# Loads of the late modulation one step ahead, a fifth raw buffer, and earlier splits of weight tiles

## The chip, the cores and the metric

The kernel runs on one core of a Trainium2 chip. The metric is the device time of one execution in microseconds; the time of a kernel is the median of its runs. Engine names: TensorE (PE in the profile; PEld is its load of the stationary operand), VectorE (DVE), ScalarE (ACT), GpSimd (POOL, not used here) and SyncE (SP, which only issues DMAs here).

## The reference

One layer of a diffusion backbone in float32, for 256 latent tokens x and 256 context tokens, model width 2048. A conditioning vector c gives six modulation rows of 2048, three for the mixer and three for the feed-forward part:

```
sh_m, sc_m, g_m, sh_f, sc_f, g_f = split(silu(c) @ w_ada + b_ada, 6)
h = rmsnorm(x, norm_mix_w) * (1 + sc_m) + sh_m
p = h @ w_in                       # 2048 x 13376: x, B, C, dt | z | pool | fourier | three gates
merged = g0 * pool(p) @ w_pool * pool_scale + g1 * fourier(p) @ w_fourier + g2 * ssd(p) @ w_ssd_out
x = x + g_m * (merged @ w_out)
h2 = rmsnorm(x, norm_ffn_w) * (1 + sc_f) + sh_f
x = x + g_f * ((silu(h2 @ w_gate) * (h2 @ w_up)) @ w_down)     # d_ff = 5632
out = rmsnorm(x, final_norm_w)
```

`ssd` is a bidirectional Mamba-2 scan (32 heads of 64, state 128, chunks of 128) that starts from the context's final states; `pool` is a box mean over a 4 x 64 grid with windows 2 to 16; `fourier` is the real part of a two-dimensional DFT over positions and channels of a group.

## The kernel before, in words

**Products in three parts.** Each float32 operand is split into a high part (a cast to fp32r) and a low part (the rest). A product is three matmuls, high by high, high by low and low by high (L143 to L145). Weights come in tiles of 512 KB, two blocks of 128 rows by 512 columns, into a `raw` tile (L128 `stage_raw`). ScalarE casts the high half `whi` (L124), VectorE subtracts to get the low half `wlo` (L125), and twelve 128x512 matmuls use the tile. There are four `raw` buffers and three each of `hi` and `lo`. `raw` buffers are also used for the tiles of w_ada, for `stage_h` (L913) and for the last pieces of the down product (L1021).

**Stages.** Up to some 135 us the kernel computes the mixer's modulation, normalises and modulates the tokens and projects B, dt and the first columns of x. Then comes the mixer, whose steps are written in the string `ORDER`: u and P (pooling), x, c, s (SSD of one of four groups), z (its gate), F and f (Fourier), p, Y, q. After it come the output projection, the second norm (`norm_ffn`, L883) with the order on TensorE written out by hand, five rounds of `gate_up` (L972), a `down` over what they made, and so on to the last norm.

**The late modulation.** Of the six modulation rows, four (SC_F, SH_F, G_M, and later G_F) aren't needed by the mixer. `ada_rest` (L344) is a generator that computes them beside the projections: one step loads a 512 KB tile of w_ada, 128 rows by 1024 columns, into a `raw` buffer and adds it, scaled by a column of silu(c), to an accumulator `adacc` on VectorE (L355; the first of sixteen steps is a plain product). Sixteen steps make one half of a row; then follow a split, a sum over partitions on TensorE, and a bias. There are 96 steps for the first three rows, and 32 for G_F, which starts in `gate_up(0)`. `proj` and the other projections call `bg(n)` after each weight tile; n is a fraction from the table `BG`, and one step is run when the fractions reach one, so about every second or third weight tile.

**What sets the order.** The kernel's code gives the program order, and a scheduler that runs before the launch orders the instructions of TensorE, VectorE, ScalarE and SP from it: an instruction that comes earlier in the program has priority over a later one where both can be issued. Engines execute their instructions in the order that results. `load` (L97) issues a DMA on SP only after the last weight load in program order; weight loads themselves stay in their order. A load waits for the release of its buffer, and so do all loads behind it on SP. TensorE's order is fixed by hand only in the output projection and the norm behind it.

**The SSD step.** For each group, two halves of four heads (b) and two token tiles (t), `ssd` builds four `rh` tiles (L557 ScalarE, L559 VectorE), multiplies them with triangular constants (L560 `rh,gt_r` and `rh,lt_r`), takes the exponential E (L563), multiplies it into W (L569), multiplies W with x (L572 `W,xl`), adds the skip (L577 `yT`) and transposes the result (L582 `cc,yT`). `rh` has QR = 4 buffers. The Fourier step reads two tables (L97 `t<-ftab`), first used on TensorE at L796; the pooling step reads `ptab` (used at L759).

Of the kernel before, what the change touches and what calls it, by code (L numbers as in the profile page):

```python
# [11 lines left out]
F32 = mybir.dt.float32  # L12
# [52 lines left out]
WORK_AT = (0, 1, 8)  # L65
FETCH, STAGE, AT_W = 8, 1, 4

QR, QE = 4, 1
APART, APART2, TURNS0, TURNS1 = 3, 3, 1, 1
ORDER = "u P x0 c x1 u s0 x2 s1 z0 F x3 P z1 s2 p0 F z2 p1 f0 s3 z3 p2 f1 Y f2 p3 q0 f3 q1 q2 q3"  # L70
BG = {"x": 0.5, "z": 0.5, "u": 0.5, "p": 0.35, "F": 0.35, "f": 0.35, "q": 0.35, "s": 0.45}


@with_exitstack
def hybrid_block(ctx: ExitStack, tc, io):
# [51 lines left out]
    def stage_raw(src, n=CH):  # L127
        raw = wp.tile([P, 2, n], F32, tag="raw", name=nm("raw"), bufs=4)  # L128
        last[0] = nc.sync.dma_start(raw, src)
        return raw  # L130

    def stage(src, n=CH, raw=None):
        raw = raw or stage_raw(src, n)
        hi = wp.tile([P, 2, n], F32R, tag="hi", name=nm("whi"), bufs=3)
        lo = wp.tile([P, 2, n], F32R, tag="lo", name=nm("wlo"), bufs=3)
        split(hi, lo, raw)
        return hi, lo
# [8 lines left out]

    # ---------------------------------------------------------------- constants
    pp = C([P, PP_N], nme="pp")
# [40 lines left out]

    # ---------------------------------------------------------------- input norms  # L190
    xnT = [H([P, 2, CH], nme="xnT") for _ in range(8)]
# [37 lines left out]

    # ---------------------------------------------------------------- modulation of the mixer, B and dt  # L230
    Am = C([P, KT, 2], nme="Am")
# [58 lines left out]
    def project_bc(b):  # L290
        """B, dt and the first columns of x of quantum b, in steps"""
        hi, lo = stage(None, CH, w_raw[b][0])
        xhi, xlo = stage(None, 256, w_raw[b][1])
        yield

        def part(out, h, l, cs):
            for k in range(2):
                kt = 2 * b + k
                mm3(out, h[:, k, cs], l[:, k, cs], hh[b][:, k, :], hl[b][:, k, :], kt == 0, kt == KT - 1)

        for ct in range(4):
            part(bacc_[ct], hi, lo, slice(ct * P, (ct + 1) * P))
            yield
        for k in range(2):
            kt = 2 * b + k
            w = dtp[kt // 8][:, kt % 8, :]
            T.matmul(dtps, w, hh[b][:, k, :], start=kt == 0, stop=False)
            T.matmul(dtps, w, hl[b][:, k, :], start=False, stop=kt == KT - 1)
        yield
        for ct in range(2):  # L310
            part(xacc0[ct], xhi, xlo, slice(ct * P, (ct + 1) * P))
            yield
# [4 lines left out]
    nc.sync.dma_start(dtw, rows(w_in, 0, KT, DT_OFF, 64))  # L317
    # the parts of the columns of dt side by side: upper, lower
    dtp = [H([P, 8, P], F32R, nme="dtp") for _ in range(2)]
# [16 lines left out]

    # ---------------------------------------------------------------- background: rest of the modulation
    Af = C([P, KT], nme="Af")
# [4 lines left out]

    def ada_rest(offs):  # L344
        for off in offs:
            for half in range(2):
                a = wp.tile([P, 1024], F32, tag="adacc", name=nm("adacc"), bufs=1)
                for kt in range(KT):
                    raw = wp.tile([P, 1024], F32, tag="raw", name=nm("raw"), bufs=4)
                    c0 = off + half * 1024  # L350
                    load(raw, w_ada[kt * P : (kt + 1) * P, c0 : c0 + 1024])
                    if kt == 0:
                        V.tensor_scalar(a, raw, sil[:, kt : kt + 1], None, ALU.mult)
                    else:
                        V.scalar_tensor_tensor(a, raw, sil[:, kt : kt + 1], a, ALU.mult, ALU.add)  # L355
                    yield
# [40 lines left out]

    # ---------------------------------------------------------------- convolution
    def conv(dst, src, ct, ns):
        """dst, src: (P, ns, 256); depthwise taps of channel tile ct, then silu."""  # L400
        o = Q([P, ns, 256], nme="cv")
        w = [cwh[:, 5 * ct + k : 5 * ct + k + 1] for k in range(5)]
        S.activation(o, src, AF.Identity, bias=cwh[:, 120 + ct : 121 + ct], scale=w[2])
        for k in (1, 3, 0, 4):
            d = k - 2
            a, b = max(0, -d), 256 - max(0, d)
            V.scalar_tensor_tensor(o[:, :, a:b], src[:, :, a + d : b + d], w[k], o[:, :, a:b], ALU.mult, ALU.add)  # L407
        t = Q([P, ns, 256], nme="cvt")
        S.activation(t, o, AF.Tanh)
        V.scalar_tensor_tensor(dst, t, 1.0, o, ALU.add, ALU.mult)  # L410
# [7 lines left out]

    # ---------------------------------------------------------------- dt, decays
    def cs(ap):  # L420
# [56 lines left out]

    # ---------------------------------------------------------------- B, C
    BT = [H([P, 2, 2, 256], nme="BT") for _ in range(2)]
# [3 lines left out]

    # ---------------------------------------------------------------- SSD
    def bh(ap, n):
# [101 lines left out]

    # ---------------------------------------------------------------- token-major projections
    def h_op(kt, t):
# [154 lines left out]

    # ---------------------------------------------------------------- pooling
    dh, dl = [], []
# [25 lines left out]

    # ---------------------------------------------------------------- Fourier
    tabs = []
# [56 lines left out]

    # ---------------------------------------------------------------- output projection, residual
    def to_feature(chunks, scale=None, colscale=None):
        """(P, 2, CH) token-major chunks to split feature-major (P, 4, 256) tiles."""
        oh, ol = [], []
# [34 lines left out]
    def norm_ffn(t):  # L870
        """scales the rows of token tile t; returns four functions that turn and modulate them"""
        if t == 0:
# [37 lines left out]

    # the last columns and the first of the next product: the norm of one token tile under the products of the other
    def stage_h(w, p, c0):
        raw = wp.tile([P, 2, CH], F32, tag="raw", name=nm("raw"), bufs=4)  # L913
        hi, lo = H([P, 2, CH], F32R, nme="hhi"), H([P, 2, CH], F32R, nme="hlo")
# [53 lines left out]

    # ---------------------------------------------------------------- SwiGLU
    ah, al = [None] * NFC, [None] * NFC  # L970
# [33 lines left out]

    def down(n0, n1):
        for n in range(4):
            ps = proj(io["w_ffn_down"], 4 * n0, 4 * (n1 - n0), n * CH, pair_op(ah[n0:n1], al[n0:n1]))
# [11 lines left out]
    for n in range(4):  # L1019
        for p in range(2):  # L1020
            raw = wp.tile([P, 2, CH], F32, tag="raw", name=nm("raw"), bufs=4)  # L1021
            hi, lo = H([P, 2, CH], F32R, nme="dhi"), H([P, 2, CH], F32R, nme="dlo")
# [118 lines left out]
```

## Time and profile before

| what | value |
|---|---|
| runs | 1921.07, 1922.86, 1921.36 us |
| median | 1921.36 us |
| span of the profiled execution | 1922.6 us |
| granted TensorE clock, mean | 0.990 |
| HBM read | 405.56 MB, 212 GB/s over the span with what is written |

Times in the profile are microseconds from the start of the span. A row of a group gives line, engine, operation, output and inputs, the count, then busy time, mean nanoseconds of one, and the idle time just before with what ended most of it. A row of the waits gives who waited, for what, the total in us, how often, and the longest. A row of the windows gives a stretch, its length, the busy time of each engine with its count, the granted clock (1 is full speed), the share of DMA time and the rate. A row of the timeline gives start, duration, what ran, and in brackets the idle time before it and what ended it. Matmuls are pipelined, so the bars of two that follow overlap.

### The profile page before, as it was taken

The page shows a single profiled execution, that of the slowest core. Times are in us where ns is not written, and L with a number is a line of the kernel's source. Part 1 is how long each engine was busy: PE and PEld are TensorE (multiplying, and loading weights), DVE is VectorE, ACT ScalarE, POOL GpSimd, SP SyncE. Part 2 cuts the span into 40 slices and gives each one's busy share as a digit, 9 for nine tenths or more (in the row PEclk, how much of TensorE's full clock was granted, in tenths as well). Part 3 has the DMA queues.
Part 4 walks back from the last instruction along what each step waited for, and adds up shares of the span by engine and source line. Part 5 has one row for each costly group of instructions (what it writes and reads, how often), then busy time and mean ns, then how long its engine had stood idle before and what let it go on. Part 6 is the DMA issues. An engine that isn't in the chain of part 4 may idle for free.

```text
span 1922.6 us, 23276 instructions
## 1 busy us (share of the span) xinstructions
PE 1847.1 (96%) x8804; PEld 1483.4 (77%) x8804; DVE 1236.8 (64%) x1515; ACT 852.5 (44%) x1177; POOL 0.2 (0%) x4
## 2 busy tenths in 40 slices
PE   5999999999999999999999999999999999999998
PEld 3677886867777768777877887787788888888886
DVE  4338869695886687766656657666655555555567
ACT  5225535464464454533434544443343444433444
POOL 0000000000000000000000000000000000000000
PEclk8999999999999999999999999999999999999999
DMA  9985745454656747677777665787766666656655
GB/s 333 353 288 158 243 145 167 142 155 158 186 157 208 248 152 252 216 250 247 244 248 245 201 226 152 256 277 260 247 211 191 196 188 186 191 192 196 187 186 175
DMA packets 214081, 409.19 MB, mean 213 GB/s; under 512 B 14801, under 2 KB 51793, under 8 KB 213969
## 3 DMA queue, kind: packets, MB, share of 16 engines
q1 hardware_dynamic: 213968, 407.71, 67.1%
q8 instruction: 69, 1.13, 0.3%
q14 instruction: 44, 0.35, 0.1%
HBM read 405.56 MB, written 2.10 MB: 212 GB/s over the span
## 4 chain that ended last, share of the span: by engine, by line
PE 66%; DMA 17%; DVE 11%; issue 4%; ACT 2%; DVEq 0%; SPq 0%; ACTq 0%
PE acc L144 19%; PE acc L145 19%; PE acc L143 19%; DMA raw<-w_ada 14%; DVE wlo L125 5%; DVE adacc L355 2%; PE aux L262 1%; DVE cv L407 1%; PE aux L560 1%; DMA t<-ptab 1%; PE aux L522 1%; DMA raw<-w_in 1%; ACT whi L124 1%; PE aux L759 1%; DMA psc<-pool_scale 1%
## 5 line engine op out<-in xcount | busy, mean ns | idle before, releaser
L124 ACT CAST whi<-raw 128x1024 fp32r<-128x1024 f32 (+1 forms) x553 | 574.2, 1040 | 799.5 <-PE acc L145 554.2
L125 DVE TENSOR_TENSOR wlo<-raw,whi 128x1024 fp32r<-128x1024 f32 (+1 forms) x553 | 662.3, 1207 | 354.2 <-ACT whi L124 353.3
L144 PE MATMUL acc<-wlo,h2h 128*128 128x512 f32 x704 | 275.4, 391 | 2.5 <-DVE wlo L125 2.5
L143 PE MATMUL acc<-whi,h2h 128*128 128x512 f32 x704 | 275.0, 391 | 2.3 <-ACT h2h L124 2.3
L145 PE MATMUL acc<-whi,h2l 128*128 128x512 f32 x704 | 275.4, 391 | 0.0
L355 DVE SCALAR_TENSOR_TENSOR adacc<-raw,sil,adacc 128x1024 f32<-128x1024 f32 x120 | 154.0, 1283 | 176.1 <-DMA raw<-w_ada 175.8
L144 PE MATMUL acc<-wlo,lh 128*128 128x512 f32 x512 | 201.8, 394 | 5.4 <-DVE wlo L125 5.4
L143 PE MATMUL acc<-whi,lh 128*128 128x512 f32 x512 | 201.3, 393 | 0.0
L145 PE MATMUL acc<-whi,ll 128*128 128x512 f32 x512 | 200.6, 392 | 0.0
L144 PEld LDWEIGHTS acc<-wlo,h2h 128*128 128x128 f32 x704 | 132.4, 188 | 30.9 <-DVE wlo L125 3.8
L143 PEld LDWEIGHTS acc<-whi,h2h 128*128 128x128 f32 x704 | 132.3, 188 | 29.6 <-ACT h2h L124 2.7
L145 PEld LDWEIGHTS acc<-whi,h2l 128*128 128x128 f32 x704 | 132.5, 188 | 28.2 <-DVE h2l L125 1.3
L145 PE MATMUL acc<-whi,al 128*128 128x512 f32 x320 | 124.7, 390 | 0.0
L144 PE MATMUL acc<-wlo,ah 128*128 128x512 f32 x320 | 124.7, 390 | 0.0
L143 PE MATMUL acc<-whi,ah 128*128 128x512 f32 x320 | 124.6, 389 | 0.0
L144 PEld LDWEIGHTS acc<-wlo,lh 128*128 128x128 f32 x512 | 96.1, 188 | 29.9 <-DVE wlo L125 9.9
L145 PE MATMUL acc<-hh,wlo 128*128 128x512 f32 x288 | 113.8, 396 | 0.8 <-DVE wlo L125 0.8
L144 PE MATMUL acc<-hl,whi 128*128 128x512 f32 x288 | 114.5, 398 | 0.0
L143 PE MATMUL acc<-hh,whi 128*128 128x512 f32 x288 | 112.1, 402 | 0.9 <-ACT whi L124 0.9
L143 PEld LDWEIGHTS acc<-whi,lh 128*128 128x128 f32 x512 | 96.1, 188 | 20.7 <-issue 0.8
L145 PEld LDWEIGHTS acc<-whi,ll 128*128 128x128 f32 x512 | 96.1, 188 | 19.8 <-issue 0.2
L145 PEld LDWEIGHTS acc<-whi,al 128*128 128x128 f32 x320 | 60.1, 188 | 12.4
(294 smaller groups left out, 2467.8 us busy)
## 6 DMA issues: line engine op xcount, KB each, us to landing
raw<-w_in SPq DMA_DIRECT2D x200, 512.0 KB, 4.6
raw<-w_ada SPq DMA_DIRECT2D x192, 512.0 KB, 5.1
raw<-w_ffn_gate SPq DMA_DIRECT2D x88, 512.0 KB, 4.4
raw<-w_ffn_up SPq DMA_DIRECT2D x88, 512.0 KB, 4.4
raw<-w_ffn_down SPq DMA_DIRECT2D x88, 512.0 KB, 4.1
raw<-w_ssd_out SPq DMA_DIRECT2D x32, 512.0 KB, 4.9
raw<-w_out SPq DMA_DIRECT2D x32, 512.0 KB, 4.2
raw<-w_fourier SPq DMA_DIRECT2D x16, 512.0 KB, 4.5
```

Source lines behind the costliest of these rows:

```text
L124: S.copy(hi, src)
L125: V.tensor_tensor(lo, src, hi.bitcast(F32), ALU.subtract)
L143: T.matmul(out, ah, bh, start=first, stop=False)
L144: T.matmul(out, ah, bl, start=False, stop=False)
L145: T.matmul(out, al, bh, start=False, stop=last)
L262: T.matmul(ps[32 * k : 32 * k + 32, o], stat[:, 4 * p + k, :], raws[8 * j + i][:, k, :], start=p == 0, stop=p == 3)
L355: V.scalar_tensor_tensor(a, raw, sil[:, kt : kt + 1], a, ALU.mult, ALU.add)
L407: V.scalar_tensor_tensor(o[:, :, a:b], src[:, :, a + d : b + d], w[k], o[:, :, a:b], ALU.mult, ALU.add)
L522: T.matmul(ps, btk[:, 2 + t, :], xc[d][t], start=t == 0, stop=t == 1)
L560: T.matmul(seg, m, rh, start=n == 0, stop=n == 3)
L759: T.matmul(ps[:, k, :], u_pool[c][:, t, cc_ * P : (cc_ + 1) * P], tb[:, i, t, :], start=t == 0, stop=t == 1)
```

## The change

Five things, as they stand in the code:

1. The `raw` tag has five buffers, in all four places that allocate it.
2. `stage` puts its split under a scheduling priority 400 instructions ahead, so that the scheduler ranks it as if it stood that much earlier in the program. The splits of the late modulation, of `stage_h` and of the last pieces are not under it.
3. `ada_rest` asks for its tile one step ahead: the first step only loads, each later one loads the next tile and accumulates the one before.
4. `rh` has three buffers, and `BG["s"]`, the fraction in `gate_up`, goes from 0.45 to 0.48.
5. `down` runs what is left of the late modulation first.

```
-QR, QE = 4, 1
+AHEAD = 400
+QR, QE = 3, 1
...
-BG = {"x": 0.5, "z": 0.5, "u": 0.5, "p": 0.35, "F": 0.35, "f": 0.35, "q": 0.35, "s": 0.45}
+BG = {"x": 0.5, "z": 0.5, "u": 0.5, "p": 0.35, "F": 0.35, "f": 0.35, "q": 0.35, "s": 0.48}
...
-        raw = wp.tile([P, 2, n], F32, tag="raw", name=nm("raw"), bufs=4)
+        raw = wp.tile([P, 2, n], F32, tag="raw", name=nm("raw"), bufs=5)
...
-        split(hi, lo, raw)
+        with tc.high_priority(offset=AHEAD):
+            split(hi, lo, raw)
...
     def ada_rest(offs):
+        units = [(off, half, kt) for off in offs for half in range(2) for kt in range(KT)]
+        coming = []
+
+        def ask():
+            off, half, kt = units.pop(0)
+            c0 = off + half * 1024
+            coming.append(wp.tile([P, 1024], F32, tag="raw", name=nm("raw"), bufs=5))
+            load(coming[-1], w_ada[kt * P : (kt + 1) * P, c0 : c0 + 1024])
+
+        ask()
+        yield
         for off in offs:
             for half in range(2):
                 a = wp.tile([P, 1024], F32, tag="adacc", name=nm("adacc"), bufs=1)
                 for kt in range(KT):
-                    raw = wp.tile([P, 1024], F32, tag="raw", name=nm("raw"), bufs=4)
-                    c0 = off + half * 1024
-                    load(raw, w_ada[kt * P : (kt + 1) * P, c0 : c0 + 1024])
+                    if units:
+                        ask()
+                    raw = coming.pop(0)
                     if kt == 0:
...
     def down(n0, n1):
+        for _ in rest:
+            pass
```

The lines of the changed kernel are 1 to 13 higher than those of before (L355 becomes L368, L125 becomes L126, L560 becomes L573, L572 becomes L585, L582 becomes L595).

**VectorE in the late mixer,** in the first `ssd_out` step. Names end in the number of a buffer's tile; the same tile has a number smaller by one in the changed kernel. On SP the w_ada tile 7610 is loaded behind the weight tiles 7556, 7574 and 7592, and 7673 behind 7613, 7631 and 7655, in both kernels. Before:

```order
L355 SCALAR_TENSOR_TENSOR adacc_7369<-raw_7553,sil_96,adacc_7369 128x1024
L125 TENSOR_TENSOR wlo_7559<-raw_7556,whi_7558 128x1024
L125 TENSOR_TENSOR wlo_7577<-raw_7574,whi_7576 128x1024
L355 SCALAR_TENSOR_TENSOR adacc_7369<-raw_7610,sil_96,adacc_7369 128x1024
L125 TENSOR_TENSOR wlo_7595<-raw_7592,whi_7594 128x1024
L125 TENSOR_TENSOR wlo_7616<-raw_7613,whi_7615 128x1024
L355 SCALAR_TENSOR_TENSOR adacc_7369<-raw_7673,sil_96,adacc_7369 128x1024
L125 TENSOR_TENSOR wlo_7634<-raw_7631,whi_7633 128x1024
```

The same place in the changed kernel:

```order
L368 SCALAR_TENSOR_TENSOR adacc_7431<-raw_7552,sil_96,adacc_7431 128x1024
L126 TENSOR_TENSOR wlo_7558<-raw_7555,whi_7557 128x1024
L368 SCALAR_TENSOR_TENSOR adacc_7431<-raw_7609,sil_96,adacc_7431 128x1024
L126 TENSOR_TENSOR wlo_7576<-raw_7573,whi_7575 128x1024
L126 TENSOR_TENSOR wlo_7594<-raw_7591,whi_7593 128x1024
L126 TENSOR_TENSOR wlo_7615<-raw_7612,whi_7614 128x1024
L368 SCALAR_TENSOR_TENSOR adacc_7431<-raw_7672,sil_96,adacc_7431 128x1024
L126 TENSOR_TENSOR wlo_7633<-raw_7630,whi_7632 128x1024
```

The accumulation of tile 7610 (now 7609) stood behind the low half of 7574 and now stands before it. The load of 7673 waited for the buffer of 7610, four tiles before it; that of 7672 waits for the buffer of 7591, five tiles before it, which the low half two rows ahead of its accumulation frees.

**TensorE at the end of the SSD step s1.** `acc` rows are the projection that runs beside it; sixteen more of them stand between the last `rh,lt_r` and the first row here. Before:

```order
L143 MATMUL acc_3502<-whi_3638,hh_1205 128x512
L144 MATMUL acc_3502<-wlo_3639,hh_1205 128x512
L572 MATMUL aux_3251<-W_3308,xl_3094 64x128 x4
L145 MATMUL acc_3502<-whi_3638,hl_1206 128x512
L143 MATMUL acc_3502<-whi_3638,hh_1205 128x512
L144 MATMUL acc_3502<-wlo_3639,hh_1205 128x512
L145 MATMUL acc_3502<-whi_3638,hl_1206 128x512
L143 MATMUL acc_3503<-whi_3638,hh_1205 128x512
L582 MATMUL aux_3325<-cc_73,yT_3322 128x128
```

In the changed kernel:

```order
L146 MATMUL acc_3502<-wlo_3638,hh_1205 128x512
L147 MATMUL acc_3502<-whi_3637,hl_1206 128x512
L573 MATMUL aux_3286<-rh_3302,lt_r_112 128x512
L585 MATMUL aux_3250<-W_3307,xl_3093 64x128 x4
L595 MATMUL aux_3324<-cc_73,yT_3321 128x128 x4
L145 MATMUL acc_3722<-hh_379,whi_3728 128x512
L146 MATMUL acc_3722<-hl_380,whi_3728 128x512
```

The projection's matmuls that stood between the last three steps of the SSD are now ahead of them, and its last tile is through when the SSD's end begins.

**SP around the Fourier tables,** somewhat later in the same step. Before:

```order
L129 DMA raw_3796<-w_in 128x2x512
L97 DMA raw_3830<-w_ada 128x1024
L129 DMA raw_3833<-w_in 128x2x512
L97 DMA t_3657<-ftab 128x512
L97 DMA t_3658<-ftab 128x1024
L129 DMA raw_3865<-w_in 128x2x512
L97 DMA raw_3926<-w_ada 128x1024
```

In the changed kernel:

```order
L130 DMA raw_3795<-w_in 128x2x512
L98 DMA raw_3829<-w_ada 128x1024
L130 DMA raw_3832<-w_in 128x2x512
L130 DMA raw_3864<-w_in 128x2x512
L98 DMA raw_3898<-w_ada 128x1024
L130 DMA raw_3901<-w_in 128x2x512
L130 DMA raw_3933<-w_in 128x2x512
L98 DMA t_3656<-ftab 128x512
L98 DMA t_3657<-ftab 128x1024
```

Three weight tiles and one tile of w_ada now stand ahead of the tables that stood behind them.

More of the change, by code (lines that the diff above doesn't have):

```diff
@@ L912, in stage_h @@
     def stage_h(w, p, c0):
-        raw = wp.tile([P, 2, CH], F32, tag="raw", name=nm("raw"), bufs=4)
+        raw = wp.tile([P, 2, CH], F32, tag="raw", name=nm("raw"), bufs=5)
         hi, lo = H([P, 2, CH], F32R, nme="hhi"), H([P, 2, CH], F32R, nme="hlo")
@@ L1020, in hybrid_block @@
         for p in range(2):
-            raw = wp.tile([P, 2, CH], F32, tag="raw", name=nm("raw"), bufs=4)
+            raw = wp.tile([P, 2, CH], F32, tag="raw", name=nm("raw"), bufs=5)
             hi, lo = H([P, 2, CH], F32R, nme="dhi"), H([P, 2, CH], F32R, nme="dlo")
```

## Prediction

> **What bounds the kernel now.** I read the busy times first, then the costliest groups and the landing of the DMAs.
>
> ```profile
> span 1922.6 us, 23276 instructions
> ...
> PE 1847.1 (96%) x8804; PEld 1483.4 (77%) x8804; DVE 1236.8 (64%) x1515; ACT 852.5 (44%) x1177; POOL 0.2 (0%) x4
> ...
> L125 DVE TENSOR_TENSOR wlo<-raw,whi 128x1024 fp32r<-128x1024 f32 (+1 forms) x553 | 662.3, 1207 | 354.2 <-ACT whi L124 353.3
> ...
> L355 DVE SCALAR_TENSOR_TENSOR adacc<-raw,sil,adacc 128x1024 f32<-128x1024 f32 x120 | 154.0, 1283 | 176.1 <-DMA raw<-w_ada 175.8
> ...
> raw<-w_ada SPq DMA_DIRECT2D x192, 512.0 KB, 5.1
> ```
>
> TensorE is busy for 96% of the span, so whatever the change does to the loads, it can only move the other 4% and the stretches in which TensorE runs slowly. VectorE spends 176 us waiting for w_ada in front of the late modulation's accumulation (L355), a load that takes 5.1 us. That is the wait which the change goes for. How much of it reaches TensorE is the question, so the waits come next: one row of VectorE, then those of TensorE behind the first phase.
>
> ```profile
> DVE adacc L355 <- DMA raw<-w_ada: 175.8, 82, 4.9
> ...
> PE acc L144 <- DVE wlo L125: 16.3, 21, 1.7
> ...
> PE aux L992 <- DVE sg L985: 6.0, 4, 3.0
> PE aux L759 <- DMA t<-ptab: 5.8, 2, 3.5
> ...
> PE aux L522 <- DVE xc L516: 2.5, 1, 2.5
> ...
> PE aux L802 <- ACT pq L797: 2.2, 1, 2.2
> PE aux L368 <- ACT adasb L367: 2.2, 1, 2.2
> PE aux L796 <- DMA t<-ftab: 2.0, 1, 2.0
> ```
>
> 82 waits of VectorE, 175.8 us, leave 21 waits of TensorE for a low half (L125) and 16.3 us; four more (6.0 us) are for the SwiGLU's product on VectorE (L985). Seven eighths of VectorE's wait is hidden by split tiles in store. Last, the windows say where TensorE's idle time lies.
>
> ```profile
> core 0: us, PE busy (x) PEld busy (x) DVE busy (x) ACT busy (x) POOL busy (x), PEclk, DMA share, GB/s
> 135.00:300.00 165.00, 158.87 (x812) 133.09 (x805) 130.05 (x171) 77.43 (x110) 0.00 (x0) 0.98 0.59 179
> 300.00:440.00 140.00, 133.78 (x613) 99.46 (x612) 116.28 (x175) 77.56 (x162) 0.00 (x0) 1.00 0.51 153
> 560.00:700.00 140.00, 132.70 (x600) 104.40 (x599) 92.53 (x104) 57.16 (x78) 0.00 (x0) 0.99 0.69 219
> 800.00:1075.00 275.00, 266.14 (x1173) 215.91 (x1172) 170.99 (x164) 112.46 (x119) 0.00 (x0) 1.00 0.75 246
> 1180.00:1365.00 185.00, 176.45 (x780) 144.01 (x780) 126.13 (x121) 76.73 (x82) 0.00 (x0) 0.99 0.81 261
> 1365.00:1900.00 535.00, 535.00 (x2388) 442.31 (x2388) 301.09 (x294) 223.13 (x226) 0.00 (x0) 1.00 0.65 198
> ```
>
> From 1365 us on TensorE has no gap: 535 us in which nothing is to be had. TensorE's idle time, span less busy, is 6.1, 6.2, 7.3, 8.9 and 8.6 us in the five other windows, 37.1 us in all. This, with the half-speed stretches below, is the most that the change can bring.
>
> **How VectorE's wait becomes TensorE's.** The timeline around 879 us shows VectorE's rows, the issue of the load on SP, and TensorE's rows.
>
> ```profile
> 884.70 1.28 DVE L355 SCALAR_TENSOR_TENSOR adacc<-raw,sil,adacc 128x1024 f32<-128x1024 f32 x1 [4.61 <-DMA raw<-w_ada]
> 885.90 3.49 DVE L125 TENSOR_TENSOR wlo<-raw,whi 128x1024 fp32r<-128x1024 f32 x3
> ```
>
> ```profile
> 878.98 0.34 SPq L97 DMA_DIRECT2D raw<-w_ada  x1
> ```
>
> ```profile
> 885.71 0.39 PE L145 MATMUL acc<-whi,yl 128*128 128x512 f32 x1
> 885.94 0.39 PE L143 MATMUL acc<-whi,yh 128*128 128x512 f32 x1
> 887.17 0.50 PE L144 MATMUL acc<-wlo,yh 128*128 128x512 f32 x1 [0.84 <-DVE wlo L125]
> ```
>
> The load is issued at 878.98; VectorE, which runs its instructions in order, stands 4.61 us at the accumulation; three low halves are queued behind it and then run in one piece; TensorE stands 0.84 us at 887.17. Matmuls start 0.23 us apart (885.71, 885.94), so a weight tile, 12 of them, feeds TensorE for 2.8 us. One wait is hidden where the store is full, and shows where two follow closely.
>
> A second price hangs on TensorE's longer waits.
>
> ```profile
> 516.85:520.26 3.41, 3.41 (x8) 2.76 (x9) 1.92 (x3) 0.59 (x2) 0.00 (x0) 0.50 0.83 269
> 687.51:690.93 3.42, 3.08 (x4) 1.51 (x5) 3.42 (x6) 0.00 (x0) 0.00 (x0) 0.50 0.41 146
> 1359.94:1363.35 3.41, 3.41 (x13) 2.80 (x12) 2.58 (x5) 1.19 (x2) 0.00 (x0) 0.50 0.89 307
> ```
>
> In these windows, behind the ptab wait (up to 3.5 us), the xc wait (2.5) and the longest sg wait (3.0), the granted clock is 0.50 for 3.41 us: half of that, 1.7 us, is lost on top of the wait. The waits of 2.2 us (L802, L368) show none. [...]
>
> **The change, part by part.**
>
> *Asking one step ahead, fifth raw buffer.* The loads keep their order on SP almost everywhere, and so does the number of steps; BG["s"] moves from 0.45 to 0.48, which brings the G_F tiles a little earlier and costs nothing but DMA time where DMA is 0.81 busy. But the accumulation does not stand later on VectorE. In the late mixer the order shown above has it one weight tile earlier: it was behind two low halves of tiles loaded before it and is now behind one. The fifth buffer thus goes to weights, and a load whose buffer comes free one tile sooner is also used one tile sooner. Take the piece shown: the load of the third w_ada tile waits for the buffer of the weight tile split two places ahead of its accumulation. The loop is two low halves (2 x 1.2), a landing (5.1), an accumulation (1.3): 8.8 us, against three weight tiles of TensorE, 3 x 2.8 = 8.4. Where the loop carries two tiles (5.6), it does not fit at all, but neither did it before:
>
> ```profile
> 949.81 1.28 DVE L355 SCALAR_TENSOR_TENSOR adacc<-raw,sil,adacc 128x1024 f32<-128x1024 f32 x1 [4.17 <-DMA raw<-w_ada]
> 951.01 3.49 DVE L125 TENSOR_TENSOR wlo<-raw,whi 128x1024 fp32r<-128x1024 f32 x3
> 958.16 1.28 DVE L355 SCALAR_TENSOR_TENSOR adacc<-raw,sil,adacc 128x1024 f32<-128x1024 f32 x1 [3.65 <-DMA raw<-w_ada]
> ```
>
> From one accumulation to the next it is 8.35 us already. I put the excess of 0.4 us on about eight such loops: **+3** in 800 to 1075. Ends: -6 (two thirds of the window's 8.9 us idle goes) and +10 (0.84 us at each of a dozen accumulations).
>
> *Priority of the splits.* Splits go ahead of VectorE's and ScalarE's other work, so a tile loaded one earlier is also split earlier. This helps where the wait came from the mixer's other work. FFN window: of 8.6 us idle and 1.7 us of half clock at 1360 I take half: **-5** (ends 0 and -10). 560 to 700: 7.3 idle and 1.7 of half clock, the xc wait among them: **-5** (0 to -9). 135 to 440: 12.3 idle, of which the table and adasb waits stay: **-4** (0 to -8). What was late stays late for sg and xc if the splits now go ahead of these too, which is why I take half and no more. Together -14.
>
> *QR 4 to 3 and the order on TensorE.* The fourth rh tile must wait for the first, and with projections drawn forward nothing is left to stand between the end of s1 and the next gating. Before:
>
> ```profile
> 426.90 0.63 PE L560 MATMUL aux<-rh,lt_r 128*128 128x512 f32 x2
> 427.37 0.40 PE L145 MATMUL acc<-whi,hl 128*128 128x512 f32 x1
> ...
> 431.57 0.66 PE L572 MATMUL aux<-W,xl 128*64 128x128 f32 x8
> ...
> 433.44 0.27 PE L582 MATMUL aux<-cc,yT 128*128 128x128 f32 x1
> ```
>
> ```profile
> 427.63 0.60 ACT L563 ACTIVATE E<-aux 128x512 f32<-128x512 f32 x1
> ```
>
> ```profile
> 430.72 0.69 DVE L569 TENSOR_TENSOR W<-W,E 128x512 f32<-128x512 f32 x1
> ```
>
> Between 427.53 and 431.57 projections cover the exponential (0.60) and the product W (0.69); between 432.23 and 433.44 five more cover yT. Afterwards lt_r, W,xl and cc,yT follow each other directly. What is then bare is 0.60 + 0.69 plus the release gaps (0.10 from 427.53, 0.16 to 431.57) plus 1.2 us up to cc,yT: 2.8 us. The order shows the same at the end of s2: **+5.5**. Ends: 0 (the covered projections are merely done earlier, and TensorE was to wait for weights anyway) and +9, with 1.7 us of half clock at each.
>
> *ftab.* The two table loads stand three weight tiles later on SP, less one for the fifth buffer: 2 x 2.8 = 5.6 us. TensorE already waits 2.0 us for them (L796). Some of the added time falls together with the bare end of s1, since both hold TensorE at the same place: 5.6 - 2.8, and half of the 1.7 us of half clock: **+4** (ends 0 and +7). [...]
>
> *The rest* costs nothing measurable: down() finds the G_F steps done or nearly so; the loads and accumulations are as many as before.
>
> Sum: -14 + 5.5 + 4 + 3 = -1.5. The profiled execution has 1922.6, so 1921.1; the profile's span is 1.2 above the median shown (1921.36), so 1919.9, about 1920.
>
> **The rivals.**
>
> *A, VectorE's wait really goes.* If loads land before the accumulation is reached, the 16.3 us behind L125 and the 6.0 at L985 go, and two half-clock episodes (3.4): 25.7; less the tails (5.5) and ftab (4), -16, 1905; without these two -26, 1896. For it: 175.8 us are waited for a load that could be asked earlier. Against: the accumulations moved up in the order. 0.28.
>
> *B, no change beyond what can be measured.* A measurement of this kernel tells about 0.2%, 3.8 us, from no change. Gains in the early mixer and the FFN meet the tails; the sum above is here, 1914 to 1927. It includes that the change doesn't do what it says, the accumulation standing as near to its load as before. 0.42.
>
> *C, slower by new waits at the end of s1.* The ends of the table term (+7) and of the tails (+9) come together at 425 to 445 and at s2, and the accumulations cost their 3: 19, with the early gains halved (-7): +12, 1922.6 - 1.2 + 12 = 1933. It decides from the point where TensorE's wait at the table passes about 2.5 us, since then the half clock follows too. For it: the order leaves no projection there. Against: it is only two places. 0.30.
>
> **How the numbers follow.** The likeliest case is B and its sum, 1920. B's own range is 1914 to 1927. For 8 in 10 the range takes in A with both new costs (from 1903, two below its 1905) and C up to two above its 1933 (1935). Faster by over 0.2%, below 1917.5: A and a quarter of B, 0.38. Slower, above 1925.2: C and a little of B, 0.32. Within: 0.30.
>
> **What would show it.** In the changed profile: VectorE's wait at the accumulation stays over 120 us (A: below 60); TensorE's wait for ftab is 4 us or more where it was 2.0; gaps of 1 to 2 us in front of W,xl and cc,yT at the end of s1 and s2; less idle at 1180 to 1365 than 8.6 us; the half clock at 687 gone. If VectorE's wait falls below 60 us, or TensorE shows no gap at the end of s1, the reasoning is wrong.

## The result and the profile after

The changed kernel takes 1945.08 us (median of six runs, 1935.54 to 1950.09) against 1922.11 for the kernel before (six runs). The ratio is estimated at 1.0105, 95% interval 1.0081 to 1.0129, which is 20 us; the two medians alone are 23 us apart. 1920 was forecast and no more than 1935 allowed for. The profiled execution has a span of 1942.5 us, 19.9 more than before.

The head of the page, and the row of the accumulation:

```profile
span 1942.5 us, 23293 instructions
...
PE 1855.7 (96%) x8804; PEld 1490.5 (77%) x8804; DVE 1237.9 (64%) x1515; ACT 853.6 (44%) x1177; POOL 0.2 (0%) x4
...
L368 DVE SCALAR_TENSOR_TENSOR adacc<-raw,sil,adacc 128x1024 f32<-128x1024 f32 x120 | 153.9, 1283 | 165.8 <-DMA raw<-w_ada 165.2
```

TensorE runs the same 8804 matmuls. It is idle for 1942.5 - 1855.7 = 86.8 us, before for 1922.6 - 1847.1 = 75.5: 11.3 us more. It is busy for 8.6 us more with the same work. The two make the 19.9. VectorE's wait for w_ada, at which the change aims, went from 175.8 to 165.2 us: the load is asked earlier and the accumulation waits nearly as long.

TensorE's waits in the changed kernel:

```profile
PE acc L146 <- DVE wlo L126: 20.8, 21, 2.7
...
PE aux L1005 <- DVE sg L998: 6.6, 3, 2.6
PE acc L145 <- ACT xin L657: 6.2, 2, 3.3
PE aux L585 <- DVE W L582: 4.5, 2, 2.8
PE aux L381 <- ACT adasb L380: 4.0, 1, 4.0
PE aux L772 <- DMA t<-ptab: 2.9, 2, 1.6
```

The waits for low halves grew from 16.3 to 20.8 us. New are two waits for `xin`, a copy by which ScalarE empties the accumulators of the x projection (6.2 us), and two for W at the end of the SSD steps (4.5); the wait for adasb went from 2.2 to 4.0. The ptab wait fell from 5.8 to 2.9, and the view has no row for ftab any more.

Most of the 8.6 us of busy time is the clock. The windows at half speed in the changed kernel between the first phase and the last norm, then two of before that the prediction didn't show:

```profile
239.80:243.20 3.40, 3.09 (x7) 2.48 (x8) 3.23 (x5) 1.94 (x4) 0.00 (x0) 0.50 0.43 122
311.50:318.30 6.80, 4.94 (x16) 4.19 (x17) 5.56 (x12) 1.25 (x3) 0.00 (x0) 0.50 0.51 167
441.20:444.60 3.40, 3.02 (x9) 2.42 (x10) 3.01 (x6) 0.81 (x2) 0.00 (x0) 0.50 0.92 336
502.60:506.00 3.40, 3.40 (x10) 2.62 (x9) 3.33 (x5) 1.05 (x1) 0.00 (x0) 0.50 0.46 141
574.30:581.10 6.80, 5.81 (x21) 4.51 (x22) 5.10 (x9) 1.47 (x4) 0.00 (x0) 0.50 0.30 115
611.90:615.30 3.40, 3.40 (x17) 3.30 (x16) 1.67 (x3) 1.03 (x4) 0.00 (x0) 0.50 0.36 84
673.30:676.70 3.40, 3.40 (x10) 2.62 (x9) 0.86 (x1) 0.73 (x1) 0.00 (x0) 0.50 0.95 311
915.60:919.00 3.40, 3.40 (x9) 2.66 (x10) 3.40 (x5) 0.00 (x0) 0.00 (x0) 0.51 0.89 301
```

```profile
172.10:175.51 3.41, 3.01 (x7) 2.44 (x8) 3.41 (x7) 0.03 (x1) 0.00 (x0) 0.50 0.26 77
196.00:199.41 3.41, 3.41 (x9) 2.70 (x9) 1.28 (x1) 0.00 (x0) 0.00 (x0) 0.50 0.71 226
```

In the changed kernel these are 34.0 us at half clock, before it was five windows of 3.4, or 17.1. TensorE is busy for 30.5 us in them, in the five of before for 16.3; half of the difference, 7.1 us, is what the granted clock of 0.50 adds by estimate, out of 8.6. So a wait with a half clock behind it is paid twice: as idle time, and as slow work.

Where the 20 us arise is read from places that both kernels pass: the second ptab use, the first waiting matmul of norm_y, and the wait for h2h at the start of the feed-forward part. Before, then the changed kernel:

```profile
516.80 3.68 PE L759 MATMUL aux<-t,u 128*128 128x256 f32 x8 [3.50 <-DMA t<-ptab]
...
789.57 0.44 PE L735 MATMUL aux<-cc,y 128*128 128x128 f32 x2 [1.02 <-DVE yl L738]
...
1172.86 0.50 PE L143 MATMUL acc<-whi,h2h 128*128 128x512 f32 x1 [2.33 <-ACT h2h L124]
```

```profile
524.72 2.64 PE L772 MATMUL aux<-t,u 128*128 128x256 f32 x11 [1.57 <-DMA t<-ptab]
...
807.01 0.44 PE L748 MATMUL aux<-cc,y 128*128 128x128 f32 x2 [0.71 <-DVE yl L751]
...
1196.03 0.50 PE L145 MATMUL acc<-whi,h2h 128*128 128x512 f32 x1 [2.35 <-ACT h2h L125]
```

The changed kernel is 7.9 us late at the table, 17.4 at norm_y, 23.2 at the feed-forward part, and 19.9 at the end. All that stands ahead of the feed-forward part loses 23 us; the feed-forward part gains 3.

### The profile page after: what moved, and what is told of

Its sections match the earlier page's. It is cut to its first block, busy times and chain, and to the rows that moved or that the text cites. A ratio compares the mean times of both kernels' runs of the same rounds, so it can differ in the third digit from the quotient of the medians.

```text
span 1942.5 us, 23293 instructions
## 1 busy us (share of the span) xinstructions
PE 1855.7 (96%) x8804; PEld 1490.5 (77%) x8804; DVE 1237.9 (64%) x1515; ACT 853.6 (44%) x1177; POOL 0.2 (0%) x4
## 4 chain that ended last, share of the span: by engine, by line
PE 65%; DMA 17%; DVE 11%; issue 4%; ACT 2%; SPq 0%; DVEq 0%; ACTq 0%
PE acc L146 19%; PE acc L147 19%; PE acc L145 19%; DMA raw<-w_ada 15%; DVE wlo L126 5%; DVE adacc L368 2%; PE aux L264 1%; DVE cv L420 1%; ACT whi L125 1%; PE aux L573 1%; DMA t<-ptab 1%; PE aux L535 1%; PE aux L585 0%; PE aux L1005 0%; PE aux L772 0%
## 5 line engine op out<-in xcount | busy, mean ns | idle before, releaser
L125 ACT CAST whi<-raw 128x1024 fp32r<-128x1024 f32 (+1 forms) x553 | 574.9, 1041 | 835.2 <-PE acc L147 698.9
L126 DVE TENSOR_TENSOR wlo<-raw,whi 128x1024 fp32r<-128x1024 f32 (+1 forms) x553 | 662.1, 1207 | 368.0 <-ACT whi L125 366.8
L368 DVE SCALAR_TENSOR_TENSOR adacc<-raw,sil,adacc 128x1024 f32<-128x1024 f32 x120 | 153.9, 1283 | 165.8 <-DMA raw<-w_ada 165.2
L145 PEld LDWEIGHTS acc<-whi,ah 128*128 128x128 f32 x320 | 60.1, 188 | 12.4
```

The costliest lines, as they stand in the source:

```text
L125: S.copy(hi, src)
L126: V.tensor_tensor(lo, src, hi.bitcast(F32), ALU.subtract)
L145: T.matmul(out, ah, bh, start=first, stop=False)
```

## How a low half ahead of the convolution stops TensorE

The wait for `xin` at 240 us shows the mechanism that the prediction lacked. VectorE, ScalarE and TensorE of the changed kernel:

```profile
233.26 1.28 DVE L368 SCALAR_TENSOR_TENSOR adacc<-raw,sil,adacc 128x1024 f32<-128x1024 f32 x1
234.62 1.23 DVE L126 TENSOR_TENSOR wlo<-raw,whi 128x1024 fp32r<-128x1024 f32 x1
235.77 3.10 DVE L420 SCALAR_TENSOR_TENSOR cv<-xin,cwh,cv 128x510 f32<-128x510 f32 x4
```

```profile
238.96 0.63 ACT L422 ACTIVATE cvt<-cv 128x512 f32<-128x512 f32 x1 [4.37 <-DVE cv L420]
239.49 0.57 ACT L657 COPY xin<-acc 128x512 f32<-128x512 f32 x1
```

```profile
240.11 0.80 PE L145 MATMUL acc<-hh,whi 128*128 128x512 f32 x1 [2.89 <-ACT xin L657]
```

An accumulation and a low half stand ahead of four taps of the convolution (L420) on VectorE. ScalarE has gone on to the tanh behind these taps (L422) and stands there for 4.37 us; behind it in its queue is the copy (L657) that frees an accumulator, and TensorE waits for that. The copy itself takes 0.57 us. The taps' input was ready at 233.64, when ScalarE had made their first term (L416); they began 2.1 us later, 0.9 of it for the rest of the accumulation and 1.2 for the low half.

The other wait for `xin`, at 501 us, has another cause:

```profile
495.90 1.29 DVE L368 SCALAR_TENSOR_TENSOR adacc<-raw,sil,adacc 128x1024 f32<-128x1024 f32 x1 [3.58 <-DMA raw<-w_ada]
...
497.19 3.09 DVE L420 SCALAR_TENSOR_TENSOR cv<-xin,cwh,cv 128x510 f32<-128x510 f32 x4
```

```profile
501.53 0.50 PE L145 MATMUL acc<-whi,lh 128*128 128x512 f32 x1 [3.30 <-ACT xin L657]
```

No low half holds these taps up. VectorE stands for 3.58 us at an accumulation whose load hasn't landed, and the taps behind it, whose input was ready at 493.34, start at 497.19.

At the end of s1 a low half stands ahead of W: VectorE does it (1.23 us from 438.45) and only then the product with E, for which TensorE stands until 440.34:

```profile
438.45 1.23 DVE L126 TENSOR_TENSOR wlo<-raw,whi 128x1024 fp32r<-128x1024 f32 x1
439.60 0.69 DVE L582 TENSOR_TENSOR W<-W,E 128x512 f32<-128x512 f32 x1
```

```profile
437.18 0.39 PE L573 MATMUL aux<-rh,lt_r 128*128 128x512 f32 x1
440.34 0.66 PE L585 MATMUL aux<-W,xl 128*64 128x128 f32 x8 [2.77 <-DVE W L582]
441.58 1.29 PE L595 MATMUL aux<-cc,yT 128*128 128x128 f32 x4 [0.58 <-DVE yT L590]
```

E (L576) was ready at 438.92, so the low half makes 0.7 of these 2.77 us. A cast that ScalarE did ahead of E makes another 0.7 (lt_r ends at 437.57, E starts at 438.33). The rest is the bare chain.

## The experiments

The theories: **P**, the priority of the splits costs the time, since they overtake short steps on which TensorE depends; **Q**, three rh buffers serialise the SSD; **R**, the accumulations still stand in front of their loads, with low halves behind them, and no earlier request mends that. Each ratio is to the kernel before, with its 95% interval.

**The change without the priority.**

```
-        with tc.high_priority(offset=AHEAD):
-            split(hi, lo, raw)
+        split(hi, lo, raw)
```

> The changed kernel without the scheduling priority of the weight splits; everything else of the change stays. Theory P (the priority puts casts and subtractions ahead of the short steps that TensorE waits for, and draws projections ahead of the SSD's end): the loss goes, 1915 to 1926 us, and TensorE shows no wait above 2.5 us at xin (L657's copy), at W,xl or at adasb. Theory Q (three rh buffers serialise the end of the SSD steps): still 1935 or more. Theory R (the accumulations, asked one step ahead, follow each other too closely and the fifth buffer doesn't help them): still 1932 to 1945, with the loss in 800 to 1075.

Measured: 1.0040 (1.0023 to 1.0057), 1931.15 us, which lies in none of the three ranges. P accounts for 0.65 of the 1.05%, not for all. In its profile the W wait has shrunk to 0.5 us and adasb to 1.3, but one wait for xin of 3.4 us is still there. It is the one that was at 501 us, behind a waiting accumulation, so that one is not the priority's:

```profile
PE acc L144 <- ACT xin L656: 3.4, 1, 3.4
```

**The priority alone,** on the kernel before.

```
+        with tc.high_priority(offset=AHEAD):
+            split(hi, lo, raw)
-        split(hi, lo, raw)
```

> The kernel before with the priority of the weight splits alone: four raw buffers, four rh buffers, w_ada loaded in its own step. Theory P: 1935 to 1950 us, with TensorE waits for xin or W of 2 to 4 us and more stretches at a clock of 0.50 than the five of before. Theories Q and R: as before, 1918 to 1926.

Measured: 1.0051 (1.0028 to 1.0074), 1935.74 us. The priority costs half a per cent by itself, with 3.4 us of W waits in its profile (two, the longest 3.1) and none for xin.

**Five raw and three rh buffers alone,** then **three rh buffers alone.**

```
-QR, QE = 4, 1
+QR, QE = 3, 1
...
-        raw = wp.tile([P, 2, n], F32, tag="raw", name=nm("raw"), bufs=4)
+        raw = wp.tile([P, 2, n], F32, tag="raw", name=nm("raw"), bufs=5)
```

> The kernel before with five raw and three rh buffers (both go together, since five raw with four rh don't fit the memory); no priority, no asking ahead. Theory P: no loss, 1914 to 1924. Theory Q: 1930 to 1940, from waits at rh and W. Theory R: as before or better, since no load is asked ahead: 1912 to 1922.

> The kernel before with three rh buffers instead of four, nothing else. Theory P: 1919 to 1927, the SSD steps being covered by projections still. Theory Q: 1930 to 1940. Theory R: 1919 to 1927.

Measured: 1.0033 (1.0011 to 1.0055) for both, 1.0015 (0.9999 to 1.0031) for three rh alone. Q falls: three rh buffers are hardly to be told from four. They do bring short W waits (three, 3.2 us together, none above 1.1). All the buffers together cost a third of a per cent, where no loss was expected by P. Their 1930.13 us lie in the range that Q had given, but not by Q's waits: W makes 0.5 us, rh none. What grew is TensorE's wait for low halves, 24.5 us against 16.3. The version without priority has these buffers and the asking ahead; it stands at 1.0040. So asking one step ahead, by itself, is worth nothing that these intervals show.

**The priority only from the feed-forward part on,** and **only ahead of it.** The split is under the priority if a flag is set (or not set), and the first gate_up sets it.

```
+        if ffn[0]:
+            with tc.high_priority(offset=AHEAD):
+                split(hi, lo, raw)
+        else:
+            split(hi, lo, raw)
```

> The changed kernel with the priority only from the first gate_up on; splits of the mixer have none. Theory P1 (the priority costs its time in the mixer alone, where casts and low halves overtake the short steps of convolution and SSD): the ratio to before falls from the 1.0105 of the whole change to that without any priority or lower, 1.000 to 1.004. Theory P2 (the priority costs its time wherever it is, by splitting too early and filling the hi and lo buffers): 1.005 to 1.010.

> The changed kernel with the priority only up to the first gate_up. Theory P1: as slow as the whole change, 1.008 to 1.013. Theory P2: 1.004 to 1.007.

Measured: 1.0011 (0.9993 to 1.0028) and 1.0152 (1.0128 to 1.0175). In the mixer the priority costs 0.9% (1.0105 against 1.0011) to 1.1% (1.0152 against 1.0040), 18 to 21 us; in the feed-forward part it brings 0.3% (1.0040 against 1.0011) to 0.5% (1.0152 against 1.0105), just clear of the intervals. That is P1, and the loss in the mixer is above what it had asked for: the whole change is the sum of a loss and a smaller gain.

**The priority on ScalarE's cast alone.**

```
+        with tc.high_priority(offset=AHEAD):
+            S.copy(hi, raw)
+        V.tensor_tensor(lo, raw, hi.bitcast(F32), ALU.subtract)
```

> The changed kernel with the priority on ScalarE's cast alone; VectorE's subtraction keeps its place in the program. If the loss comes from subtractions that overtake VectorE's short steps (the convolution's taps, W times E), it falls to that without priority: 1.003 to 1.006, and the 3 us waits at xin go. If it comes from the casts on ScalarE, it stays: 1.009 to 1.013.

Measured: 1.0037 (1.0016 to 1.0058), as without any priority. So the loss needs the priority of the subtraction on VectorE; that of the cast alone costs nothing that shows. The priority of the subtraction alone was not run, and whether it costs more by what it overtakes on VectorE or by the projections that it draws forward on TensorE isn't separated. The wait for W at the SSD's end is 0.3 us here against 4.5, and one xin wait is left, the one that the version without priority has too:

```profile
PE acc L146 <- ACT xin L658: 3.5, 1, 3.5
```

**The priority also on the convolution of x.** Its copy, taps and tanh in project_x go under the same priority.

```
+            with tc.high_priority(offset=AHEAD):
+                if ct in cts:
+                    b = Q([P, 2, 256], nme="xin")
...
+                conv(xs[ct // 2][:, ct % 2], b, 4 * g + ct, 2)
```

> The changed kernel with the same priority also on the convolution of x (its copy, taps and tanh), so that the splits no longer rank ahead of these. If the waits at xin come from that overtaking, those two (6.5 us in the profile of the changed kernel, and 3.4 us of half clock) go, and the ratio is 1.003 to 1.007; the waits at the end of the SSD steps stay. If not, 1.009 to 1.013.

Measured: 1.0064 (1.0038 to 1.0091). The ratio is as expected, the waits only in part. Of the two xin waits, the one that was at 240 us fell from 2.89 to 0.80; the one behind a waiting accumulation stayed at 3.21, and the expectation was wrong to put it down to the overtaking. adasb fell to 1.3, and W stayed (5.6 us), as it should:

```profile
PE acc L145 <- ACT xin L658: 4.0, 2, 3.2
```

**The accumulation held behind a low half,** in the changed kernel without priority. The subtraction that `stage` made last is remembered, and the accumulation is to be issued after it.

```
-        split(hi, lo, raw)
+        last_lo[0] = split(hi, lo, raw)
...
+                        with tc.issue_after(last_lo[0].ins):
+                            V.scalar_tensor_tensor(a, raw, sil[:, kt : kt + 1], a, ALU.mult, ALU.add)
```

> The changed kernel without the priority, and each accumulation of a w_ada tile bound to stand behind the low half of the weight tile that was last staged when it is written, so that it can't move up towards its load. Theory R (the accumulation still waits for its load because the scheduler lets it move up): VectorE's wait at the accumulation falls from 161 to below 80 us, and the time falls below the kernel before, 1905 to 1918 us, ratio 0.991 to 0.998. Rival S (the fifth buffer and the DMA order bring the loss, not the accumulation's place): the wait falls, but the ratio stays at 1.002 to 1.006.

**The same on the kernel before:** load in the same step, four buffers each, no priority.

> The kernel before with only that order of the accumulation added: load in the same step, four raw buffers, four rh buffers, no priority. Theory R: VectorE's wait falls a little, to 110 to 160 us, since the load is issued but one tile ahead, and the ratio is 0.995 to 1.000. Rival S: no change, 0.999 to 1.001, whatever the wait does.

Measured: 1898.70 us, 0.9853 (0.9836 to 0.9871), and 1899.49 us, 0.9859 (0.9842 to 0.9876). Both beat both kernels, and by more than R had asked. The rows of the accumulation, of the first and of the second:

```profile
L369 DVE SCALAR_TENSOR_TENSOR adacc<-raw,sil,adacc 128x1024 f32<-128x1024 f32 x120 | 153.4, 1278 | 0.0
```

```profile
L357 DVE SCALAR_TENSOR_TENSOR adacc<-raw,sil,adacc 128x1024 f32<-128x1024 f32 x120 | 153.5, 1279 | 0.6 <-DMA raw<-w_ada 0.5
```

The 175.8 us are gone even where the load isn't asked ahead. The second version, in VectorE's timeline and on SP:

```profile
875.27 1.22 DVE L126 TENSOR_TENSOR wlo<-raw,whi 128x1024 fp32r<-128x1024 f32 x1 [1.41 <-ACT whi L125]
878.07 1.22 DVE L126 TENSOR_TENSOR wlo<-raw,whi 128x1024 fp32r<-128x1024 f32 x1 [1.58 <-ACT whi L125]
879.22 1.28 DVE L357 SCALAR_TENSOR_TENSOR adacc<-raw,sil,adacc 128x1024 f32<-128x1024 f32 x1
```

```profile
872.76 0.34 SPq L98 DMA_DIRECT2D raw<-w_ada  x1
```

From its issue at 872.76 the load has 6.46 us until the accumulation at 879.22, more than the 4.9 that such a load takes in this version; two low halves are done in between. VectorE's pauses are now short ones for ScalarE's casts. The windows of this version where the loads are densest:

```profile
800.00:1075.00 275.00, 274.02 (x1223) 226.40 (x1222) 179.16 (x169) 118.08 (x123) 0.00 (x0) 1.00 0.77 252
1180.00:1365.00 185.00, 184.03 (x825) 151.30 (x824) 133.06 (x124) 78.94 (x83) 0.00 (x0) 1.00 0.84 272
```

TensorE is idle for 1.0 and 1.0 us where it was for 8.9 and 8.6. My expectation for the second version was a small gain, on the view that a load asked in the same step couldn't be early enough. That was wrong: a load of 5 us (4.9 here, 5.1 before) needs about two weight tiles of 2.8 us, and the order alone gives them.

**Both together.** The whole change with its priority and the held accumulations; then the held accumulations with the priority in the feed-forward part alone.

> The whole change with its priority, and the accumulations bound behind the low half last staged. If the two causes are separate (theories P1 and R both), the priority costs here what it costs elsewhere, 0.5 to 0.65% on top of 0.985: 0.990 to 0.993, with VectorE's wait at the accumulation near nothing, and the waits at xin and at the end of the SSD steps still there. If the priority only hurts because accumulations and splits stand too close (R alone), 0.985 to 0.988.

> The version with late accumulations and without priority, and the priority in the feed-forward part alone. Theory P1 with what the priority brought there (some 0.3%, 6 us, in the comparison of two versions with early accumulations): if that came from waits that the late accumulation has removed already, no change from 0.985: 0.984 to 0.987; if it is a gain of its own, 0.981 to 0.983.

Measured: 0.9886 (0.9858 to 0.9913) and 0.9871 (0.9846 to 0.9897), against 0.9853 with no priority. The first lies between what the two theories expected and its interval reaches into both, so whether the priority costs as much there stays open, and so does which of its waits are left. In the second the priority brings nothing that shows: what it gained in the feed-forward part seems to have been time lost behind waiting accumulations, which are gone.

## Why the prediction was wrong

**Right.** That the accumulation moves up with its load and VectorE's wait stays: 175.8 to 165.2 us. That the feed-forward part gains: the changed kernel catches up 3.3 us (23.2 late at its start, 19.9 at its end), and the split of the priority shows 0.3 to 0.5%. But the idle time of its window, 8.6 us, fell only to 7.5 and not by half; the waits for sg stayed, as the prediction had feared. That the late mixer loses a little: its idle time in the window went from 8.9 to 13.6 us, where +3 was forecast. The last row is this window; the first three belong to the step that failed:

```profile
135.00:300.00 165.00, 158.53 (x824) 132.83 (x823) 129.39 (x169) 76.32 (x109) 0.00 (x0) 0.99 0.58 180
300.00:440.00 140.00, 132.51 (x592) 98.66 (x590) 114.61 (x170) 76.52 (x160) 0.00 (x0) 0.98 0.51 158
560.00:700.00 140.00, 128.88 (x579) 103.53 (x578) 85.54 (x99) 62.36 (x99) 0.00 (x0) 0.95 0.64 200
800.00:1075.00 275.00, 261.41 (x1140) 211.00 (x1141) 171.32 (x171) 111.56 (x123) 0.00 (x0) 0.99 0.73 240
```

**The step that failed** is the priority's gain in the mixer: "560 to 700 ... -5" and "135 to 440 ... -4", with ends of 0 on the other side. The window 560 to 700 is idle for 11.1 us instead of 7.3, and its clock fell from 0.99 to 0.95; 135 to 440 is idle for 14.0 us instead of 12.3. The runs put the priority in the mixer at a loss of 0.9 to 1.1%, 18 to 21 us. The prediction had 9 us of gain there, and 5.5 of loss at the bare tails, which belong to the priority too: it was 21 to 24 us too low, about the whole miss. The prediction named the danger ("What was late stays late for sg and xc if the splits now go ahead of these too") and priced it as a gain that doesn't come. But VectorE takes its instructions in order, and ScalarE behind it too (at 239.49 the copy of 0.57 us came only behind a tanh that had waited 4.37 us): a low half of 1.2 us ahead of a short step delays all that hangs on that step, and of TensorE's nine waits of 2.2 to 4 us in the changed kernel (from 135 us on) six brought a half clock as well. The two ranges ended at 0, so a loss was not even allowed for.

**The tails were mis-sized.** +5.5 was for the bare chain of E, W and yT at two places. s1 cost 2.77 + 0.58 of idle time, 3.4; at s2 the timeline below shows three waits, for rh, W and yT, 3.7 together. The idle time is 7.1 us, near the estimate of 5.5, but the low half that had slipped in makes part of it, and half of the three half-clock windows behind the two, 5.1 us, comes on top. The upper end of 9 was too low by 3. Of the two causes that the part named, three rh buffers and projections drawn forward, the first is not it: the version with these buffers and no priority has 0.5 us of W waits, three rh buffers alone have none above 1.1, and the priority with four rh buffers has one of 3.1.

```profile
572.45 0.49 PE L573 MATMUL aux<-rh,lt_r 128*128 128x512 f32 x1 [1.38 <-DVE rh L572]
574.71 1.12 PE L585 MATMUL aux<-W,xl 128*64 128x128 f32 x8 [1.76 <-DVE W L582]
576.41 0.48 PE L595 MATMUL aux<-cc,yT 128*128 128x128 f32 x1 [0.58 <-DVE yT L590]
```

**ftab was wrong:** +4 was forecast, and its wait of 2.0 us is gone. The load is issued at 440.13 (before at 433.05), and TensorE, held at the bare end of s1 until 440.34 and at half clock behind it, reaches the tables only at 445.65, without a wait. The prediction said itself that the two lie at one place, but took only 2.8 us off for it; the larger hides the other.

**Rival A's price was right and its cause wrong.** 26 us were put on VectorE's wait going, without the new costs (1896); the held accumulations make it go and give 1898.7, with TensorE idle for 20.5 us less than before and busy for 4.3 less, where A had 22.3 and 3.4. But the wait was not a matter of asking earlier: the later place of the accumulation brings all of the gain, the early request none that is measured (0.9853 with it, 0.9859 without).

**Rival C had the right sign.** It priced the table and the tails at 16 us and halved the gains; its 1933 is 12 us short of 1945.08, and of its two places only the tails were one.

**What stays open:** why five raw with three rh buffers cost 0.33% while the accumulations stand early, when the two held versions, one with these buffers and one without, take the same time. Their profile shows one place: at 151 us VectorE stands 3.33 us at an accumulation, where before it is 0.47, a second accumulation and a reciprocal of 3.34 us follow ahead of the next low half, and TensorE waits 3.70 us for that. Open is also which part of the mixer's 18 to 21 us is xin, adasb, W or the low halves, since the runs of one kernel scatter by 7 to 10 us either way.

## What to carry to other kernels

When an in-order engine waits for a DMA in front of work that is ready, first move the wait behind that work, which alone gave 0.9859 here; asking for the load earlier brought nothing here (1.0040 with it, 1.0033 without), where a scheduler moved its user up as well. A priority for the work that feeds TensorE cost time here, 0.9 to 1.1% in the mixer, where short steps that TensorE also waits for share the engine: look at what each prioritised instruction overtakes, and follow the queue of the next engine behind it. And price every new wait of TensorE of about 2 us or more with the half clock it may bring: in the changed kernel six of the nine of 2.2 to 4 us brought 3.4 or 6.8 us at 0.50.

## What the runs showed of the hardware

The length of a wait doesn't decide alone whether a half clock follows it. In the changed kernel the wait for pq, which ended at 611.49, was 1.9 us and the half clock follows at 611.9; the wait for h2h of 2.35 us at 1196 brought none. The adasb wait of 4.0 us and the three waits at s2, 3.7 us in 5, brought 6.8 us each. Between the first phase and the last norm each half clock in the traces of before and of the changed kernel lasts 3.4 or 6.8 us.

In these traces the half clock goes with how a wait falls into steps of 3.413 us. The five half-clock windows of before start at 172.10, 196.00, 516.85, 687.51 and 1359.94, which is 7, 101, 151 and 348 times 3.413 us (1187.84 / 348) behind the first. Counted on in such steps, the wait for h2h, 2.4 us in the version without priority and 2.35 in the changed kernel, lies in one step in the former (first row, the half clock behind it in the second) and is divided between two in the latter (third row):

```profile
1175.43:1178.85 3.42, 1.11 (x10) 0.91 (x9) 3.35 (x10) 1.23 (x2) 0.00 (x0) 1.00 0.00 0
1178.85:1182.26 3.41, 3.37 (x10) 2.75 (x11) 2.03 (x4) 0.98 (x2) 0.00 (x0) 0.50 0.00 0
```

```profile
1192.11:1195.52 3.41, 1.57 (x15) 1.38 (x13) 3.36 (x9) 0.78 (x2) 0.00 (x0) 1.00 0.00 0
```

TensorE is idle for 2.31 us of the first and for 1.84 of the third. In the profiles of before and of the changed kernel, between 135 and 1890 us, eleven steps at full clock were idle for 2.0 us or more (2.07 to 3.36), and a half clock followed each of them; it followed none of those at full clock that were idle for less than 1.4 us. Between the two both occur: 1.86 us brought one (pq), 1.84 us none (h2h).
